# Weight sums of the down projections: made inside DRAM by copies and accumulating transfers, in place of VectorE in SBUF

## The chip, the cores and the metric

The kernel runs on one core of a Trainium2 chip. The core has TensorE (PE, with its weight loads shown apart as PEld), VectorE (DVE), ScalarE (ACT), GpSimd (POOL) and SyncE (SP). In this kernel SP only issues transfers between DRAM and SBUF; POOL does a little arithmetic and can issue transfers too. Each engine works through its own instructions in order and waits for the others at semaphores. The metric is the time of one execution on the device in microseconds, the median of several runs.

## The reference, cut to what matters

A trunk of two layers on a sequence of 1,024 tokens with 1,024 channels. Layer 0 mixes tokens by a gated linear recurrence with 8 heads (HGRN2), layer 1 by attention in a window. Each layer ends with a gated feed-forward part, whose last step is a product with `ffn_w_out`, of 2,816 rows and 1,024 columns:

```python
def conv_ffn(h, w_in, conv_w, conv_b, w_out):
    u = h @ w_in
    ...
    a, b = jnp.split(u, 2, axis=-1)
    return (jax.nn.silu(a) * b) @ w_out
```

Each head of the recurrence ends with a normalisation over its channels:

```python
    o = o * lax.rsqrt(jnp.mean(jnp.square(o), -1, keepdims=True) + RMS_EPS)
```

## The kernel before, in words

**The product with `ffn_w_out`.** It is a Strassen-Winograd product: both matrices are cut into 2 x 2 blocks, and 7 block products stand for 8, at the price of sums of blocks on both sides. Of the weight's four blocks the method needs four sums. They depend on the weights alone, so the kernel makes them at its beginning, long before the first down projection, and keeps them in two DRAM tensors `bsd`, one for each layer, of 128 x 11 x 2 x 1,024 numbers. The class `Down` reads them back (`sum_b`, L560 to L562). `operands` (L564) loads the two operands of a product and forms the activations' sums on VectorE, then splits both into a high and a low part; `evacuate` (L610) adds a product, when it is done, into the output rows `Y`. The products come in the order 1, 2, 5, 6, 7, 3, 4.

**The stage in which the sums are made.** It is the loop over the 8 heads of layer 0. For each head TensorE makes the projections (L194 to L196 and L739, L740) and, put between them, the head's own chain of small products (L200): VectorE multiplies decays into the head's tensors level by level (L1015 to L1020), PE makes scores of them, and so on. At the end of a head's chain VectorE forms `og` (L1111), ScalarE sums its squares (L1123), GpSimd makes 1/rms of them in two small instructions (L1124, L1125), VectorE multiplies it into `og` (L1127), and PE transposes the result (L204).

The order of this stage is written out by a planner, the class `Order`: `t` counts TensorE's time as products are recorded, `v` is the time to which VectorE is booked. A chain goes on when `t` has passed the wait that it gave with `yield`; `od.behind` gives a wait until VectorE's booked work is done. Where VectorE is booked less than 1.5 us ahead, `od.fill` (the function `lay`, L1158) puts in work that can stand anywhere: low parts of weights, and the sums of `ffn_w_out`. The engines themselves know nothing of `t`: on the chip each takes its instructions in the recorded order as soon as their semaphores allow.

**The sums.** `slot_begin` (L1188) is called at the begin of each of 64 slots (8 for each head). The weight is cut into 22 units of 256 rows, 11 for each layer. A slot stores the units that are summed (SP, L1193), loads the next unit into two free rows of `Y` (SP, two transfers, L1200), and puts the four subtractions of a unit loaded two slots ago into `pending`, from which `lay` takes them one by one (VectorE, L1209):

```python
for x, y, z in ((b11, b12, b11), (b12, b22, b12), (b22, b22, b11), (b21, b21, b22)):
    pending.append(lambda x=x, y=y, z=z: tt(x, y, z, op=sub))
```

The same SP queue carries the weights of the heads (L164, tiles `raw`), which ScalarE (L176) and VectorE (L169) split into a high and a low part in `HL`.

Of the kernel before, what the change touches and what calls it, by code (L numbers as in the profile page):

```python
# [107 lines left out]
def trunk(ctx: ExitStack, tc: tile.TileContext, a: dict, out: bass.AP):  # L108
# [429 lines left out]
    class Down:  # L538
# [25 lines left out]
        def operands(self, i, k):  # L564
# [10 lines left out]
            elif p == 5:  # L575
                self.block_a(R[:, 0], k, 1, 0)
                self.block_a(x[:, 0], k, 1, 1)
                self.sum_b(R[:, 1], k, 1)
                tt(R[:, 0], R[:, 0], x[:, 0], op=add)
                x = R  # L580
            elif p == 6:
                self.block_a(x[:, 0], k, 0, 0)
                self.sum_b(R[:, 1], k, 2)
                tt(R[:, 0], R[:, 0], x[:, 0], op=sub)
                x = R
            elif p == 7:
                self.block_a(x[:, 0], k, 1, 1)
                self.sum_b(x[:, 1], k, 3)
                tt(x[:, 0], x[:, 0], R[:, 0], op=sub)
            elif p == 3:  # L590
                self.block_a(x[:, 0], k, 0, 1)
                self.block_b(x[:, 1], k, 1, 1)
                tt(x[:, 0], x[:, 0], R[:, 0], op=sub)
            else:
                self.block_a(x[:, 0], k, 1, 1)
                self.sum_b(x[:, 1], k, 4)
# [13 lines left out]
        def evacuate(self, p, tb, ps, ln):  # L610
            lo, hi = [Y[:, t, :].rearrange("p (h n) -> p h n", h=2) for t in (tb, tb + 4)]
            both = ps.unsqueeze(1).to_broadcast([P, 2, 512])
            if p == 1:
                for y in (lo, hi):
                    nc.vector.scalar_tensor_tensor(y, y, ALPHA, both, op0=ALU.mult, op1=ALU.add)
            elif p in (6, 7):
                tt(hi, hi, both, op=add)
            for y in {2: [lo[:, 0]], 5: [lo[:, 1], hi[:, 1]], 6: [lo[:, 1]], 3: [lo[:, 1]], 4: [hi[:, 0]]}.get(p, []):
                tt(y, y, ps, op=add)

# [57 lines left out]
    with tc.tile_pool(name="t", bufs=1, reuse_waits="tile") as raws, hgrn_pool as hp:  # L678
# [463 lines left out]

        pairs = FF // 256
        lead = [0, 3, 2, 2, 2, 2, 1, 0]
        begins = [4] + [8 * h + lead[h] for h in range(1, NH)]
        free, units, loaded, summed = {r: 0 for r in (0, 2, 4, 6)}, list(range(2 * pairs)), [], []
        slot_no = [-1]
        pending, lowparts, movelows, old = [], [], [], []

# [8 lines left out]
        def lay():  # L1158

            if lowparts and lowparts[0][0] <= od.t:  # L1160
                lay_low()
            elif pending:
                pending.pop(0)()
                od.vec(0.65, 0.0)
            elif movelows and movelows[0][1] <= od.t:
                lay_moved()
            else:
                return False
# [18 lines left out]

        def slot_begin():  # L1188
            slot_no[0] += 1
            n = slot_no[0]  # L1190
            while summed and summed[0][2] < n:
                i, r, _ = summed.pop(0)
                nc.sync.dma_start(bsd[i // pairs][:, i % pairs, :, :], Y[:, r:r + 2, :])  # L1193
                free[r] = n + 1
            rows = [r for r in free if free[r] <= n <= begins[r] + 1]
            if units and rows:
                i, r = units.pop(0), rows[0]
                for k in range(2):
                    row = (k * pairs + i % pairs) * P
                    nc.sync.dma_start(Y[:, r + k, :], a["ffn_w_out"][i // pairs][row:row + P, :])  # L1200
                loaded.append((i, r, n))
                free[r] = 9 * NH
            while loaded and loaded[0][2] <= n - 2:
                i, r, _ = loaded.pop(0)
                blocks = Y[:, r:r + 2, :].rearrange("p a (b n) -> p a b n", b=2)
                (b11, b12), (b21, b22) = [(blocks[:, k, 0], blocks[:, k, 1]) for k in range(2)]

                for x, y, z in ((b11, b12, b11), (b12, b22, b12), (b22, b22, b11), (b21, b21, b22)):
                    pending.append(lambda x=x, y=y, z=z: tt(x, y, z, op=sub))  # L1209
                last = pending.pop()  # L1210
                pending.append(lambda i=i, r=r, last=last: (last(), summed.append((i, r, slot_no[0]))))

# [17 lines left out]
        with tc.manual_schedule(engines={EN.PE, EN.SP, EN.Activation, EN.DVE, EN.Pool}):  # L1230
# [5 lines left out]
            for k in range(4):  # L1236
                slot_begin()
                next(steps)
# [12 lines left out]

            task = od.spawn(all_heads())
            w = nw
            for h in range(1, NH):
# [4 lines left out]
                for k, make in enumerate(((), make_ig[:1], make_ig[1:], ())):  # L1259
                    slot_begin()  # L1260
                    next(steps)
# [11 lines left out]
                for tp in range(NB // 2):  # L1273
                    if tp == lead[h]:
                        ready.append((h, w["out"]))
                    slot_begin()
                    if h == NH - 1 and tp:
# [8 lines left out]
                w = nw  # L1286
            if units or loaded or pending or summed:
                raise ValueError("a unit is left")
# [389 lines left out]
```

## Time and profile before

| | |
|---|---|
| median of 3 runs | 2129.04 us (2128.96 to 2129.31) |
| the profiled execution, first to last instruction | 2126.5 us |
| median less that span | 2.5 us |
| busy: PE, DVE, ACT, POOL | 2116.9, 1765.4, 926.4, 132.7 us |
| the loop over heads and its neighbourhood | 50 to 490 us of the span |
| first down projection ends | about 1160 us |
| granted TensorE clock | 0.999 |

A row of the page or of a view names the line, the engine, the operation, the output and the inputs by the program's names, the shape, and how often (`x88`); then busy time and the mean of one in ns, and what ended the idle time before. A row of the timeline begins with start and duration in us. A row of the stretches gives the stretch, its length, then busy time and number of instructions for PE, PEld, DVE, ACT and POOL, then the granted clock, the share of time in which the DMA engines were busy, and GB/s.

### The profile page before, as it was taken

How to read it: one execution, taken by the hardware profiler on the slowest of the kernel's cores; microseconds unless marked ns; L12 is line 12 of the kernel's file. 1: busy time of each engine (PE TensorE's matmuls, PEld its weight loads, DVE VectorE, ACT ScalarE, POOL GpSimd, SP SyncE). 2: the span in 40 equal slices, each digit the busy share in tenths (PEclk: the TensorE clock that was granted, in tenths of full speed). 3: DMA queues.
4: the chain of work that ended last, by engine and by line, in shares of the span. 5: the costliest groups of instructions: out<-in, count | busy, mean ns of one | idle time of the engine just before them, and what ended most of it. 6: DMA issues, size and time to landing. Idle time of an engine off the chain costs nothing.

```text
span 2126.5 us, 32114 instructions
## 1 busy us (share of the span) xinstructions
PE 2116.9 (100%) x12639; PEld 1776.7 (84%) x12639; DVE 1765.4 (83%) x2378; ACT 926.4 (44%) x1491; POOL 132.7 (6%) x150
## 2 busy tenths in 40 slices
PE   9999999999999999999999999999999999999998
PEld 8888888888888888888888888888888888888887
DVE  4777776677999999888977758969999999878986
ACT  4444444452444444444433356743544444444430
POOL 1000000001100000000001113321000000000002
PEclk9999999999999999999999999999999999999999
DMA  6655443205223222238854511042232222249662
GB/s 218 245 210 168 145 131 120 75 30 180 100 83 98 88 90 80 80 99 272 293 183 166 161 31 41 24 149 90 80 105 94 90 89 80 89 147 334 220 207 97
DMA packets 231566, 280.53 MB, mean 132 GB/s; under 512 B 30152, under 2 KB 160376, under 8 KB 228600
## 3 DMA queue, kind: packets, MB, share of 16 engines
q1 hardware_dynamic: 230464, 278.11, 39.4%
q8 instruction: 99, 1.62, 0.3%
q10 hardware_dynamic: 856, 0.37, 0.1%
q14 instruction: 51, 0.42, 0.1%
q0 software_dynamic: 96, 0.02, 0.0%
HBM read 215.51 MB, written 62.94 MB: 131 GB/s over the span
## 4 chain that ended last, share of the span: by engine, by line
PE 99%; DMA 0%; DVE 0%; SPq 0%; issue 0%; DVEq 0%; ACT 0%; ACTq 0%
PE psmm L194 17%; PE psmm L196 17%; PE psmm L195 17%; PE psax L194 10%; PE psax L195 10%; PE psax L196 10%; PE psmm L739 5%; PE psax L200 4%; PE psmm L740 3%; PE psmm L204 1%; PE psmm L200 1%; PE psax L1452 1%; PE psax L204 1%; PE psmm L1299 1%; PE psmm L777 0%; DMA raw<-in_hgrn_w_in_dram 0%
## 5 line engine op out<-in xcount | busy, mean ns | idle before, releaser
L194 PE MATMUL psmm<-T,HL 128*128 128x512 f32 x768 | 303.5, 395 | 0.0
L196 PE MATMUL psmm<-T,HL 128*128 128x512 f32 x768 | 299.4, 390 | 0.0
L195 PE MATMUL psmm<-T,HL 128*128 128x512 f32 x768 | 299.2, 390 | 0.0
L498 DVE SCALAR_TENSOR_TENSOR Y<-Y,cwt 128x1023 f32<-128x1023 f32 (+1 forms) x176 | 224.9, 1281 | 45.3 <-ACT Y L496 43.9
L221 ACT CAST HL<-rx 128x1024 fp32r<-128x1024 f32 (+1 forms) x151 | 150.7, 1007 | 174.4 <-PE psmm L195 30.4
L169 DVE TENSOR_TENSOR HL<-rx,HL 128x1024 fp32r<-128x1024 f32 (+1 forms) x151 | 178.3, 1187 | 16.5 <-ACT HL L221 16.2
L739 PE MATMUL psmm<-HL,T 128*128 128x512 f32 x496 | 176.8, 399 | 0.0
L196 PEld LDWEIGHTS psmm<-T,HL 128*128 128x128 f32 x768 | 144.2, 188 | 30.5
L194 PEld LDWEIGHTS psmm<-T,HL 128*128 128x128 f32 x768 | 144.3, 188 | 29.7 <-issue 0.4
L195 PEld LDWEIGHTS psmm<-T,HL 128*128 128x128 f32 x768 | 144.4, 188 | 28.8 <-issue 0.4
L496 ACT ACTIVATE Y<-Y,cwt 128x1024 f32<-128x1024 f32 x88 | 108.7, 1238 | 101.5 <-DVE Y L485 89.1
L740 PE MATMUL psmm<-HL,T 128*128 128x256 f32 x496 | 138.9, 280 | 0.0
L194 PE MATMUL psax<-T,HL 128*128 128x512 f32 x352 | 137.3, 390 | 0.0
L196 PE MATMUL psax<-T,HL 128*128 128x512 f32 x352 | 137.0, 389 | 0.0
L195 PE MATMUL psax<-T,HL 128*128 128x512 f32 x352 | 137.0, 389 | 0.0
L243 POOL TENSOR_TENSOR rs<-rs,nhalf 128x1 f32<-128x1 f32 x32 | 44.6, 1396 | 1287.0 <-DVE rs L242 1287.0
L739 PEld LDWEIGHTS psmm<-HL,T 128*128 128x128 f32 x496 | 93.1, 188 | 21.0
L740 PEld LDWEIGHTS psmm<-HL,T 128*128 128x128 f32 x496 | 93.7, 189 | 0.4
L221 ACT CAST HT<-rx 128x1024 fp32r<-128x1024 f32 (+1 forms) x37 | 35.5, 961 | 125.6 <-DVE rx L452 76.7
L169 DVE TENSOR_TENSOR HL<-raw,HL 128x1024 fp32r<-128x1024 f32 x51 | 62.0, 1217 | 21.4 <-ACT HL L176 20.2
L196 PEld LDWEIGHTS psax<-T,HL 128*128 128x128 f32 x352 | 66.1, 188 | 13.6
L195 PEld LDWEIGHTS psax<-T,HL 128*128 128x128 f32 x352 | 66.1, 188 | 13.6
(316 smaller groups left out, 5229.5 us busy)
## 6 DMA issues: line engine op xcount, KB each, us to landing
rx<-in_ffn_w_in_dram SPq DMA_DIRECT2D x136, 256.0 KB, 3.2
rx<-gd SPq DMA_DIRECT2D x118, 256.0 KB, 3.8
Y<-in_ffn_w_out_dram SPq DMA_DIRECT2D x44, 512.0 KB, 6.0
bsd<-Y SPq DMA_DIRECT2D x22, 1024.0 KB, 4.8
gd<-Y SPq DMA_DIRECT2D x44, 512.0 KB, 2.6
rx<-in_ffn_w_out_dram SPq DMA_DIRECT2D x54, 256.0 KB, 4.8
R<-bsd SPq DMA_DIRECT2D x44, 256.0 KB, 5.1
Y<-in_ffn_w_in_dram SPq DMA_DIRECT2D x40, 256.0 KB, 2.9
```

Of the source, the lines that this page charges most:

```text
L169: make = lambda e: e.tensor_tensor(lo, src, hi.bitcast(F32), op=ALU.subtract)
L194: nc.tensor.matmul(ps, st(0), mv(0), start=start, stop=False)
L195: nc.tensor.matmul(ps, st(0), mv(1), start=False, stop=False)
L196: nc.tensor.matmul(ps, st(1), mv(0), start=False, stop=stop)
L200: nc.tensor.matmul(ps, lhsT, rhs, start=start, stop=stop, **kw)
L204: nc.tensor.transpose(ps, src, ident)
L221: nc.scalar.copy(hi, src)
L243: nc.gpsimd.tensor_tensor(rs, rs, nhalf, op=ALU.pow)
L496: nc.scalar.activation(c, u, AF.Identity, bias=cwt[:, l, 3, ci:ci + 1], scale=cwt[:, l, 2, ci:ci + 1])
L498: nc.vector.scalar_tensor_tensor(c[:, sh:], u[:, :S - sh], cwt[:, l, 2 - sh, ci:ci + 1], c[:, sh:], op0=ALU.mult, op1=ALU.add)
L739: nc.tensor.matmul(ps, T[:, 0, kc, ts], w[:, :, kc % 4, :], start=kc == 0, stop=False)
L740: nc.tensor.matmul(ps[:, :256], T[:, 1, kc, ts], w[:, 0, kc % 4, :], start=False, stop=kc == KC - 1)
```

## The change

The four sums of a layer are made in DRAM, from `ffn_w_out` straight into `bsd`. A generator, `down_sums`, is run by the planner beside the heads. For each layer it first records four plain copies of a block, issued by SP, then in three further steps additions: GpSimd issues a transfer with `accum_op=add`, which adds its source to what stands at its destination. Each block of 11 x 128 rows goes in four pieces, of 3, 3, 3 and 2 times 128 rows; the planner books 4.5 us after each piece and 16 us more after each step.

Since these transfers add, the sums that contained differences become pure additions; that is the same method with the signs of two blocks turned, and the signs are put right elsewhere: in the activations' sums (`operands`) and when a product is added into `Y` (`evacuate`), where a product that was added to both halves of a row at once (1,024 columns with the product repeated) is now added to one half and subtracted from the other, in two instructions of 512.

The machinery of slots, units and `pending` goes, and so do the transfers of units through `Y`.

```diff
             elif p == 6:
                 self.block_a(x[:, 0], k, 0, 0)
                 self.sum_b(R[:, 1], k, 2)
-                tt(R[:, 0], R[:, 0], x[:, 0], op=sub)
+                tt(R[:, 0], R[:, 0], x[:, 0], op=add)
                 x = R
...
-            both = ps.unsqueeze(1).to_broadcast([P, 2, 512])
             if p == 1:
                 for y in (lo, hi):
-                    nc.vector.scalar_tensor_tensor(y, y, ALPHA, both, op0=ALU.mult, op1=ALU.add)
-            elif p in (6, 7):
-                tt(hi, hi, both, op=add)
-            for y in {2: [lo[:, 0]], 5: [lo[:, 1], hi[:, 1]], 6: [lo[:, 1]], 3: [lo[:, 1]], 4: [hi[:, 0]]}.get(p, []):
-                tt(y, y, ps, op=add)
+                    for c, op in enumerate((add, sub)):
+                        nc.vector.scalar_tensor_tensor(y[:, c], y[:, c], ALPHA, ps, op0=ALU.mult, op1=op)
+            for y, op in {2: [(lo[:, 0], add)], 5: [(lo[:, 1], sub), (hi[:, 1], sub)],
+                          6: [(hi[:, 0], sub), (hi[:, 1], add), (lo[:, 1], add)], 7: [(hi[:, 0], add), (hi[:, 1], sub)],
+                          3: [(lo[:, 1], sub)], 4: [(hi[:, 0], add)]}.get(p, []):
+                tt(y, y, ps, op=op)
...
-            elif pending:
-                pending.pop(0)()
-                od.vec(0.65, 0.0)
...
+        def down_sums():
+
+            n = FF // 256
+            for l in range(2):
+                wb = a["ffn_w_out"][l].rearrange("(r k p) (c n) -> r c p k n", r=2, k=n, c=2)
+                t1, t3, t4, t2 = [bsd[l][:, :, i, j * 512:(j + 1) * 512] for i in range(2) for j in range(2)]
+                steps = [((t1, wb[0, 0]), (t3, wb[1, 1]), (t2, wb[1, 1]), (t4, wb[1, 0])),
+                         ((t1, wb[0, 1]), (t3, wb[0, 1])), ((t2, t1),), ((t4, t2),)]
+                for i, step in enumerate(steps):
+                    for dst, src in step:
+                        for k0, k1 in ((0, 3), (3, 6), (6, 9), (9, n)):
+                            if i:
+                                nc.gpsimd.dma_start(dst[:, k0:k1], src[:, k0:k1], accum_op=add)
+                            else:
+                                nc.sync.dma_start(dst[:, k0:k1], src[:, k0:k1])
+                            yield 4.5
+                    yield 16.0
...
             task = od.spawn(all_heads())
+            sums = od.spawn(down_sums())
...
-            od.finish([params] + moved[:2])
+            od.finish([params, sums] + moved[:2])
```

How instructions move. On GpSimd, from the sixth head's 1/rms to the eighth's, as it stands now (`ss` is the tile of a head's sums of squares, `bsd_92` the sums of layer 1):

```order
L1124 TENSOR_SCALAR ss<-ss 128x8
L1125 TENSOR_TENSOR ss<-ss,nhalf 128x8
L1193 DMA bsd_92<-in_ffn_w_out_dram 128x3x512 x3
L1193 DMA bsd_92<-in_ffn_w_out_dram 128x2x512
L1193 DMA bsd_92<-in_ffn_w_out_dram 128x3x512 x3
L1193 DMA bsd_92<-in_ffn_w_out_dram 128x2x512
L1124 TENSOR_SCALAR ss<-ss 128x8
L1125 TENSOR_TENSOR ss<-ss,nhalf 128x8
L1193 DMA bsd_92<-bsd_92 128x3x512 x3
L1193 DMA bsd_92<-bsd_92 128x2x512
L1193 DMA bsd_92<-bsd_92 128x3x512 x3
L1193 DMA bsd_92<-bsd_92 128x2x512
```

Before, L1124 and L1125 of all eight heads followed each other with nothing between them. Now eight transfers stand behind the sixth head's pair and eight behind the seventh's; layer 0's stand behind the first head's pair (one), the second's (seven) and the third's (eight).

On VectorE, in the first head's chain, the multiplications of decays (L1015 to L1020; `qp`, `kp`, `tot` are the head's tensors, `Y` the rows that held the units of `ffn_w_out`):

```order
 L1020 TENSOR_TENSOR tot<-fg 128x512
 L1035 TENSOR_TENSOR kd<-kp,qp 128x512 x2
-L1209 TENSOR_TENSOR Y<-Y 128x512
 L1015 TENSOR_TENSOR qp<-qp,tot 128x256x2
 L1017 TENSOR_TENSOR kp<-kp,tot 128x256x2
 L1020 TENSOR_TENSOR tot<-tot 128x256
-L1209 TENSOR_TENSOR Y<-Y 128x512 x2
 L1015 TENSOR_TENSOR qp<-qp,tot 128x128x4
 L1017 TENSOR_TENSOR kp<-kp,tot 128x128x4
 L1020 TENSOR_TENSOR tot<-tot 128x128
```

The subtractions that filled VectorE between the levels of the chain are gone, and the levels follow each other directly.

On SyncE, at the begin of the second head (`raw` are the weights of the heads):

```order
 L164 DMA raw_100<-in_hgrn_w_in_dram 128x4x128 x2
-L1193 DMA bsd_91<-Y 128x2048
-L1200 DMA Y<-in_ffn_w_out_dram 128x1024 x4
-L1193 DMA bsd_91<-Y 128x2048
-L1200 DMA Y<-in_ffn_w_out_dram 128x1024 x2
+L1195 DMA bsd_91<-in_ffn_w_out_dram 128x3x512 x3
+L1195 DMA bsd_91<-in_ffn_w_out_dram 128x2x512
+L1195 DMA bsd_91<-in_ffn_w_out_dram 128x3x512 x2
 L164 DMA raw_101<-in_hgrn_w_in_dram 128x8x128
 L164 DMA raw_99<-in_hgrn_w_in_dram 128x8x128
```

Stores that waited for VectorE's sums and loads that waited for a free row of `Y` make way for six copies that depend on no engine; the next head's weights stand behind them.

More of the change, by code (lines that the diff above doesn't have):

```diff
@@ L578, in operands @@
                 self.sum_b(R[:, 1], k, 1)
-                tt(R[:, 0], R[:, 0], x[:, 0], op=add)
+                tt(R[:, 0], x[:, 0], R[:, 0], op=sub)
                 x = R
@@ L588, in operands @@
                 self.sum_b(x[:, 1], k, 3)
-                tt(x[:, 0], x[:, 0], R[:, 0], op=sub)
+                tt(x[:, 0], R[:, 0], x[:, 0], op=sub)
             elif p == 3:
@@ L592, in operands @@
                 self.block_b(x[:, 1], k, 1, 1)
-                tt(x[:, 0], x[:, 0], R[:, 0], op=sub)
+                tt(x[:, 0], R[:, 0], x[:, 0], op=sub)
             else:
@@ L1138, in norm @@
                     split_scaled(T[:, 0, h, ts], T[:, 1, h, ts], ps[:, ts], par[:, 16:17])
-        pairs = FF // 256
         lead = [0, 3, 2, 2, 2, 2, 1, 0]
[L1145 to L1148, printed above, removed]
+        lowparts, movelows, old = [], [], []
         def lay_low():
@@ L1186, in rest @@
             old[:] = soon
[L1188 to L1211, printed above, removed]
+        def down_sums():
[14 more added lines that the diff above has]
+                    yield 16.0
         def slot_end(wait, *makes):
@@ L1236, in trunk @@
             for k in range(4):
-                slot_begin()
                 next(steps)
@@ L1259, in trunk @@
                 for k, make in enumerate(((), make_ig[:1], make_ig[1:], ())):
-                    slot_begin()
                     next(steps)
@@ L1275, in trunk @@
                         ready.append((h, w["out"]))
-                    slot_begin()
                     if h == NH - 1 and tp:
@@ L1286, in trunk @@
                 w = nw
-            if units or loaded or pending or summed:
-                raise ValueError("a unit is left")
             while lowparts:
```

## The prediction

> **What bounds the kernel now.** I read the page's head and its chain first, then the waits of TensorE, then the stretch of the program in which the sums are made.
>
> ```profile
> span 2126.5 us, 32114 instructions
> PE 2116.9 (100%) x12639; PEld 1776.7 (84%) x12639; DVE 1765.4 (83%) x2378; ACT 926.4 (44%) x1491; POOL 132.7 (6%) x150
> PE 99%; DMA 0%; DVE 0%; SPq 0%; issue 0%; DVEq 0%; ACT 0%; ACTq 0%
> ```
>
> PE is busy for all but 2126.5 - 2116.9 = 9.6 us, and the chain that ended last is PE for 99%. A busy PE is modelled, so I ask next whether PE waited for anybody. This is the whole list of PE's waits over the span:
>
> ```profile
> PE psmm L834 <- DVE Y L785: 1.0, 1, 1.0
> PE psmm L777 <- ACT HL L766: 0.4, 1, 0.4
> PE psmm L777 <- DVE HL L757: 0.3, 1, 0.3
> ```
>
> All three, 1.7 us together, stand at the very start, before the loop over heads in which the sums are made. The stretch that holds this loop, from 50 to 490 us (columns: span, then busy time of PE, weight load, DVE, ACT, POOL):
>
> ```profile
> 50.00:490.00 440.00, 440.00 (x4448) 375.09 (x4447) 313.45 (x569) 196.73 (x435) 14.99 (x16) 1.00 0.43 148
> ```
>
> PE is busy for 440.00 of 440 us at a granted clock of 1.00, while DVE is idle for 126 us of it and the DMA engines for 57%. So the change works on engines that nobody waits for. Its gain is limited by what PE still waits for; its loss is whatever it makes PE wait for.
>
> **VectorE's part.** The removed subtractions, and the evacuations that are split:
>
> ```profile
> L1209 DVE TENSOR_TENSOR Y<-Y 128x512 f32<-128x512 f32 x88 | 60.1, 689 | 1.5
> L615 DVE SCALAR_TENSOR_TENSOR Y<-Y,psmm x16: 1214/1215/1222, 997.2 to 1941.0; 128x1024 f32<-128x1024 f32 x16
> L617 DVE TENSOR_TENSOR Y<-Y,psax x8: 1210/1215/1222, 1093.8 to 2030.7; 128x1024 f32<-128x1024 f32 x8
> L617 DVE TENSOR_TENSOR Y<-Y,psmm x8: 1201/1213/1220, 1118.4 to 2060.9; 128x1024 f32<-128x1024 f32 x8
> L619 DVE TENSOR_TENSOR Y<-Y,psax x24: 670/680/687, 1035.6 to 2092.3; 128x512 f32<-128x512 f32 x24
> 850.00:1160.00 310.00, 310.00 (x1373) 256.92 (x1372) 262.00 (x291) 122.45 (x126) 3.99 (x3) 1.00 0.54 181
> ```
>
> 88 subtractions of 0.689 us go, 60.1 us of DVE in the loop over heads. All of it ran beside a full PE, so it is worth 0 on the path. In the down projections 16 scaled adds and 16 plain adds of 1,024 columns become 64 of 512: 32 x (2 x 0.680 - 1.215) = 4.6 us more DVE, 2.3 us in each layer. The last row is the first layer's down projection with the last third of an up projection: DVE idles 310 - 262 = 48 us there and PE none. The extra 2.3 us is therefore hidden; if that cover were gone it would cost its 2.3 us, twice. The last products, 3 and 4, keep their instructions (a subtraction in place of an addition), so the end of a layer is as before. Sum on DVE: 1765.4 - 60.1 + 4.6 = 1709.9 us busy.
>
> The order of PE moves too, since its planner counted the subtractions as VectorE time: a head's chain of small products now stands earlier by what the planner booked for the subtractions ahead of it, 0.65 us each and up to four, 2.6 us. The same products are issued, so I take 0.
>
> **SyncE's part.** Two loads and a store for each of 22 units go, 32 copies come, mixed with the weight loads of the heads. A load can come late by what is ahead of it on the queue.
>
> ```profile
> 108.08 2.44 SPq L164 DMA_DIRECT2D raw<-in_hgrn_w_in_dram  x4
> 130.43 1.04 ACT L176 CAST HL<-raw 128x1024 fp32r<-128x1024 f32 x1
> DMA to landing us min/median/max: 2.5/3.4/6.2
> q1 hardware_dynamic: 230464, 278.11, 39.4%
> ```
>
> Loads issued by 110.5 us are first used at 130.4, 20 us later, and land in 2.5 to 6.2 us: 14 us to spare at least. The last row (packets, MB, share) gives the engines' pace: 278.11 MB in 39.4% of 2126.5 us is 332 MB per ms when all 16 work. A copy of three blocks, 128 x 3 x 2,048 bytes or 0.79 MB, is 2.4 us at that pace. At most six copies stand in a row ahead of a load: 14 us, if they all come at once. Just covered; I take 0. What the copies need they have: they wait for no engine, so SP runs ahead, and the first sum is wanted by the down projection, hundreds of us later.
>
> **GpSimd's part, which decides.** 32 accumulating transfers stand in POOL's queue, between the steps that turn a head's sum of squares into 1/rms (L1124, L1125). A transfer waits for the copy or the sum that it builds on, and behind it wait L1124, then DVE's scaling of the head (L1127), then PE's transposes (L204). POOL issues one as soon as its inputs have landed, whatever PE is doing. So each gap between two heads must hold its transfers: 1, 7, 8, 0, 0, 8, 8. These are the gaps with 7 or 8 (idle time of POOL in brackets), and the last of L1125's durations:
>
> ```profile
> 208.07 0.20 POOL L1124 TENSOR_SCALAR ss<-ss 128x8 f32<-128x8 f32 x1 [48.05 <-ACT sq L1123]
> 264.62 0.20 POOL L1124 TENSOR_SCALAR ss<-ss 128x8 f32<-128x8 f32 x1 [54.63 <-ACT sq L1123]
> 424.37 0.20 POOL L1124 TENSOR_SCALAR ss<-ss 128x8 f32<-128x8 f32 x1 [48.31 <-ACT sq L1123]
> 477.82 0.20 POOL L1124 TENSOR_SCALAR ss<-ss 128x8 f32<-128x8 f32 x1 [51.53 <-ACT sq L1123]
> 478.10 1.64 POOL L1125 TENSOR_TENSOR ss<-ss,nhalf 128x8 f32<-128x8 f32 x1
> ```
>
> What room follows, DVE's scaling and PE's first weight load of the transposes for the last two heads:
>
> ```profile
> 430.65 1.22 DVE L1127 TENSOR_TENSOR og<-og,ss 128x1024 f32<-128x1024 f32 x1
> 432.97 0.91 PEld L204 LDWEIGHTS psax<-ident,og 128*128 128x128 f32 x8
> 479.77 1.23 DVE L1127 TENSOR_TENSOR og<-og,ss 128x1024 f32<-128x1024 f32 x1 [3.30 <-POOL ss L1125]
> 484.89 1.03 PEld L204 LDWEIGHTS psax<-ident,og 128*128 128x128 f32 x8
> ```
>
> The seventh head's L1125 ends at 424.37 + 0.28 + 1.64 = 426.3: its room is 432.97 - 426.3 - 1.22 = 5.4 us. The eighth's ends at 479.74: 484.89 - 479.74 - 1.23 = 3.9 us.
>
> No accumulating transfer is in the trace. The nearest rows for its time a, with three blocks:
>
> ```profile
> bsd<-Y SPq DMA_DIRECT2D x22, 1024.0 KB, 4.8
> rx<-bsd SPq DMA_DIRECT2D x32, 256.0 KB, 2.9
> 1.24 0.78 POOL L137 DMA_DIRECT2D gd<-in_ln_mix_g_dram  x1 [0.81 <-POOLq L1661]
> 426.00:478.00 52.00, 52.00 (x548) 44.85 (x548) 40.36 (x68) 27.79 (x58) 0.47 (x2) 1.00 0.09 28
> ```
>
> Of the 2.9 us of a 256 KB load (0.26 MB), 0.8 is data at 332 MB per ms, so 2.1 is fixed; POOL's issue takes 0.8. Lower end: POOL goes on once it has issued, a = 0.8. Next: it stands until one pass over 0.79 MB has landed, 0.8 + 2.1 + 2.4 = 5.3. Upper end: the sum reads two blocks for one written, 0.8 + 2.1 + 4.7 = 7.6; a two-block piece is a - 1.5. I take 6.4, the middle of the last two: the 1,024 KB store lands in 4.8 us, and so little else uses the DMA engines in the last gap (9%) that 332, an average over packets of 1.2 KB, understates the pace. A gap of eight then keeps POOL 6a + (a - 1.5) + 0.8 = 7a - 0.7 = 44.1 us before the last is issued, under 48.31: nobody waits. At 7.6 it is 52.5: the seventh head is 4.2 us late, inside its room; the eighth 4.2 + 52.5 - 51.53 = 5.2 late, 1.3 more than its room. So the term is 0, with 1.3 at the upper end.
>
> [...]
>
> **Sum.** 2126.5 of span + 0 (DVE) + 0 (SP) + 0 (POOL) = 2126.5. The runs' median, 2129.04, lies 2.5 above this span; with that, 2129.0 us.
>
> **Rivals.** *POOL comes late (slower).* If the sum in DRAM is dearer than its bytes, L1124 waits and PE with it. From a = 7.5 the eighth head's transposes are late; with S = 7a - 0.7 the last two heads cost 2S - 103.7. At a = 8.6: S = 59.5, 15 us. The third and fourth heads add: 6a - 0.7 in a gap of 48.05, then S in 54.63, with some 3.9 us of room at the end, 13a - 107.9 = 4 us. Together 19 us: 2148. [...] For it: nothing in the trace bounds the adding. Against it: 7.5 is near the end of what bytes give, with all transfers one at a time.
>
> [...]
>
> *PE meets its chain too early (slower).* The planner now places a chain nearer to the VectorE work that it needs. Eight heads with three such places, each late by at most one 0.689 us subtraction's worth: 24 x 0.69 = 17 us, 2146. Against it: no such wait in 440 us now, and VectorE has less to do.
>
> *VectorE's relief helps PE (faster).* PE's own waits bound it at 1.7 us, 2127.3, which is less than can be told. Only if the modelled PE hides waits would it be more: with all 9.6 idle us, 2119.4.
>
> **Chances and range.** Forecast 0.77; POOL late by more than 4.3 us 0.15; chain too early 0.04; relief that shows 0.04. 0.2% is 4.3 us, about what a measurement of this kernel can tell from no change. So faster 0.04, same 0.77, slower 0.19. The range goes from the relief that the waits allow, 2127.3, to a = 8.2 in the first rival (S = 56.7, 9.7 us, the first heads nothing), 2139.0. Beyond it lie some 0.12 above and 0.04 below.
>
> **What would show it.** PE busy between 2116 and 2119 us and no PE wait for DVE L1127 or POOL in the loop over heads; DVE near 1710; L1124 starting within a few us of 208, 265, 424 and 478; the eight transfers of a gap issued over 35 to 53 us. Wrong if L1124 of the last heads ends a long POOL queue, if PE's transposes L204 show a wait, or if PE waits for a weight load behind copies.

## The result, and the profile after

| | before | after |
|---|---|---|
| median of the runs | 2129.11 us (2128.96 to 2129.31) | 2166.2 us (2163.61 to 2168.68) |
| profiled execution, first to last instruction | 2126.5 us | 2161.4 us |
| granted TensorE clock | 0.999 | 0.993 |

The ratio is 1.0174, with a 95% interval of 1.0159 to 1.0188: the change costs 37 us, where the forecast was none and its range ended at 2139.0. The two profiled executions differ by 34.9 us, and nearly all of it is lost between 173 and 525 us of before's time: PE's 101st product of L194 into `psmm` starts 0.8 us later than before, the 201st 10.6, the 301st 34.7, the last 35.2.

The page's head and chain of the changed kernel:

```profile
span 2161.4 us, 32006 instructions
PE 2126.8 (98%) x12639; PEld 1783.8 (83%) x12639; DVE 1713.3 (79%) x2322; ACT 927.1 (43%) x1491; POOL 172.6 (8%) x182
PE 87%; issue 8%; DVE 2%; POOL 2%; DMA 1%; ACT 0%; SPq 0%; DVEq 0%; POOLq 0%; ACTq 0%
```

PE is still what the time is made of, but POOL and "issue" have entered the chain, and PE's own busy time grew by 9.9 us although it issues the same 12639 products. The waits (total, how often, the longest), first PE's, then VectorE's and POOL's:

```profile
PE psax L204 <- DVE og L1127: 23.3, 3, 10.3
PE psmm L194 <- issue: 2.2, 1, 2.2
...
DVE og L1127 <- POOL ss L1125: 36.6, 4, 17.8
...
POOL bsd L1193 <- issue: 189.7, 28, 12.0
```

Read from the bottom: POOL stood 189.7 us before its transfers without waiting for any semaphore, so L1125 of a head came late, so VectorE scaled the head late, so the transposes of three heads kept PE idle for 23.3 us. The timeline of POOL shows it in place; from the third head's 1/rms to the fourth's, and the ends of the two later groups:

```profile
208.82 1.66 POOL L1125 TENSOR_TENSOR ss<-ss,nhalf 128x8 f32<-128x8 f32 x1
213.25 1.30 POOL L1193 DMA_DIRECT2D bsd<-bsd  x1 [2.77 <-issue]
220.88 1.24 POOL L1193 DMA_DIRECT2D bsd<-bsd  x1 [6.32 <-issue]
228.76 1.22 POOL L1193 DMA_DIRECT2D bsd<-bsd  x1 [6.64 <-issue]
...
271.74 1.15 POOL L1193 DMA_DIRECT2D bsd<-bsd  x1 [6.72 <-issue]
272.97 0.19 POOL L1124 TENSOR_SCALAR ss<-ss 128x8 f32<-128x8 f32 x1
...
388.75 1.29 POOL L1193 DMA_DIRECT2D bsd<-in_ffn_w_out_dram  x1
...
447.84 1.14 POOL L1193 DMA_DIRECT2D bsd<-in_ffn_w_out_dram  x1 [8.24 <-issue]
449.06 0.19 POOL L1124 TENSOR_SCALAR ss<-ss 128x8 f32<-128x8 f32 x1
449.33 1.66 POOL L1125 TENSOR_TENSOR ss<-ss,nhalf 128x8 f32<-128x8 f32 x1
454.83 1.31 POOL L1193 DMA_DIRECT2D bsd<-bsd  x1 [3.84 <-issue]
...
513.01 1.15 POOL L1193 DMA_DIRECT2D bsd<-bsd  x1 [12.03 <-issue]
514.24 0.19 POOL L1124 TENSOR_SCALAR ss<-ss 128x8 f32<-128x8 f32 x1
```

The brackets in front of L1124 that showed 48 to 55 us of idle time before are gone: POOL goes from the last transfer straight into a 1/rms that is already late. Eight transfers start over 271.74 - 213.25 = 58.5 us, then 59.1 and 58.2, one every 8.4 us. Even the first of a group waits where another group has just ended (3.84 us ahead of 454.83): the last transfer of that one, issued at 447.84, is still under way (its kind takes a median of 8.1 us to land).

The stretches around the waits of PE (stretch, length, busy time and number of PE, PEld, DVE, ACT, POOL, then the granted clock, DMA share, GB/s):

```profile
276.00:280.00 4.00, 3.78 (x15) 3.48 (x16) 3.97 (x7) 1.42 (x2) 0.00 (x0) 0.57 0.28 50
303.00:307.00 4.00, 4.00 (x12) 2.83 (x10) 0.30 (x1) 0.00 (x0) 0.00 (x0) 0.59 0.68 223
448.00:452.00 4.00, 0.00 (x0) 0.00 (x0) 0.97 (x1) 0.00 (x0) 2.83 (x3) 0.50 0.58 74
452.00:456.00 4.00, 3.69 (x15) 3.41 (x15) 3.93 (x6) 1.11 (x1) 1.17 (x1) 0.50 0.32 57
516.00:520.00 4.00, 2.51 (x10) 2.41 (x11) 1.23 (x1) 0.47 (x1) 0.18 (x1) 0.50 0.91 208
520.00:524.00 4.00, 4.00 (x14) 3.15 (x14) 1.93 (x4) 2.37 (x5) 0.00 (x0) 0.73 0.02 3
```

After these waits (4.45, 2.19, 8.60 and 10.29 us) PE works at half its clock for some us: a 512-column product then starts 0.43 us after the last, not 0.23. The clock is halved for 3.41, 3.41, 10.24 and 10.24 us at these four places, and PE works in 16.5 us of them; as an estimate, that costs 16.5 x (1 - 0.23 / 0.43) = 7.7 us, most of PE's extra 9.9 busy us. Where the rest of the 9.9 lies was not found. Waits of 23.3, a wait of 2.2 at L194 with nothing in the profile that PE waited for (read below as a wait for its own instructions, an inference whose grounds are in the last section), and 9.9 of longer work make 35.4, against 34.9 of span.

The transfers themselves, KB of each and the median from issue to landing:

```profile
bsd<-in_ffn_w_out_dram SPq DMA_DIRECT2D x24, 768.0 KB, 11.4
bsd<-in_ffn_w_out_dram POOLq DMA_DIRECT2D x12, 768.0 KB, 8.1
bsd<-bsd POOLq DMA_DIRECT2D x12, 768.0 KB, 7.5
```

### The profile page after: what moved, and what is told of

It is laid out like the page before. It is cut to its first block, busy times and chain, and to the rows that moved or that the text cites. A ratio compares the mean times of both kernels' runs of the same rounds, so it can differ in the third digit from the quotient of the medians.

```text
span 2161.4 us, 32006 instructions
## 1 busy us (share of the span) xinstructions
PE 2126.8 (98%) x12639; PEld 1783.8 (83%) x12639; DVE 1713.3 (79%) x2322; ACT 927.1 (43%) x1491; POOL 172.6 (8%) x182
## 3 DMA queue, kind: packets, MB, share of 16 engines
q0 software_dynamic: 11872, 23.09, 6.8%
q8 instruction: 99, 1.62, 0.3%
HBM read 238.58 MB, written 86.01 MB: 150 GB/s over the span
## 4 chain that ended last, share of the span: by engine, by line
PE 87%; issue 8%; DVE 2%; POOL 2%; DMA 1%; ACT 0%; SPq 0%; DVEq 0%; POOLq 0%; ACTq 0%
PE psmm L194 16%; PE psmm L196 16%; PE psmm L195 16%; PE psax L194 9%; PE psax L196 9%; PE psax L195 9%; PE psmm L739 3%; PE psax L200 2%; PE psmm L740 1%; PE psmm L200 1%; POOL bsd L1193 1%; PE psmm L204 1%; PE psax L1434 1%; PE psax L204 1%; POOL ss L1125 0%
## 5 line engine op out<-in xcount | busy, mean ns | idle before, releaser
L194 PE MATMUL psmm<-T,HL 128*128 128x512 f32 x768 | 304.2, 396 | 2.2 <-issue 2.2
L194 PEld LDWEIGHTS psmm<-T,HL 128*128 128x128 f32 x768 | 144.6, 188 | 29.7 <-issue 0.4
L194 PE MATMUL psax<-T,HL 128*128 128x512 f32 x352 | 137.3, 390 | 0.0
L194 PEld LDWEIGHTS psax<-T,HL 128*128 128x128 f32 x352 | 66.1, 188 | 13.6
## 6 DMA issues: line engine op xcount, KB each, us to landing
bsd<-in_ffn_w_out_dram SPq DMA_DIRECT2D x24, 768.0 KB, 11.4
```

What stands on the lines that cost most here:

```text
L194: nc.tensor.matmul(ps, st(0), mv(0), start=start, stop=False)
```

## The experiments

The theory after this reading: POOL lets one accumulating transfer through at a time, a group of eight keeps it some 60 us, the 1/rms behind it is late, PE waits, and runs at half clock after. The rivals: the DRAM traffic itself, or the changed order, is what costs, and POOL only shows it. Each run was timed beside runs of the kernel before on the same chip.

| run | median us | before | ratio (95%) |
|---|---|---|---|
| no accumulating transfers | 2131.08 | 2129.18 | 1.0013 (1.0003 to 1.0022) |
| more room for descriptors | 2133.37 | 2129.18 | 1.0021 (1.0012 to 1.0031) |
| transfers that copy | 2134.61 | 2129.18 | 1.0024 (1.0015 to 1.0034) |
| 1/rms on VectorE | 2133.57 | 2129.18 | 1.0021 (1.0012 to 1.0030) |
| transfers spread | 2130.58 | 2128.95 | 1.0010 (1.0001 to 1.0018) |
| spread and more room | 2131.85 | 2128.95 | 1.0016 (1.0007 to 1.0025) |
| order and signs alone | 2128.11 | 2128.95 | 0.9996 (0.9987 to 1.0005) |
| copies in one bunch | 2128.58 | 2128.95 | 0.9999 (0.9990 to 1.0008) |
| POOL held, 66 us | 2191.64 | 2129.16 | 1.0295 (1.0281 to 1.0309) |
| copies of one layer | 2128.53 | 2129.16 | 0.9997 (0.9988 to 1.0006) |
| POOL held, 59 us | 2165.78 | 2129.83 | 1.0173 (1.0159 to 1.0187) |
| POOL held as the transfers did | 2168.37 | 2129.36 | 1.0188 (1.0174 to 1.0202) |
| the extra tile alone | 2136.57 | 2129.88 | 1.0033 (1.0020 to 1.0046) |

**No accumulating transfers.** In `down_sums`:

```diff
-                                nc.gpsimd.dma_start(dst[:, k0:k1], src[:, k0:k1], accum_op=add)
+                                pass
```

> Leaves out the 32 accumulating transfers on POOL's queue (the products then use unsummed blocks); the copies on SP's queue, the turned signs and the new order on every engine stay. Theory (the 1/rms steps stand on POOL behind the transfers; PE idles for them 23.3 us, runs at a halved clock after it, about 10 us): the three waits of the transposes L204 are gone, 1/rms at the times of before, and the time is 2128 to 2133 us; the 2.2 us in which PE waited for instructions beside the copies may stay. Rival (it is the copies' traffic and PE's changed order that cost, and POOL only shows it): 2150 us or more, with waits left on PE that POOL has no part in.

35 of the 37 us are gone. What remains above before, 1.9 us, is one wait of PE:

```profile
PE psmm L194 <- issue: 1.9, 1, 1.9
PE psmm L834 <- DVE Y L785: 1.0, 1, 1.0
...
288.00:292.00 4.00, 4.00 (x160) 3.08 (x159) 0.36 (x1) 0.00 (x0) 0.00 (x0) 1.00 1.05 323
292.00:296.00 4.00, 2.15 (x10) 1.66 (x9) 3.90 (x11) 3.25 (x5) 0.00 (x0) 1.00 1.02 308
```

PE works off 160 small products and as many weight loads in 4 us, then stops, with the DMA engines full (1.05, 1.02) of the second layer's copies: it is busy for 2.15 of the next 4 us.

**More room for descriptors.** (The tile of `pr` is put in a place that is free at that time, and `sk` cut to the columns in use, to make room.) The room is `dynamic_dma_scratch_size`; what lies in it no trace shows.

```diff
-    nc = bacc.Bacc("TRN2", target_bir_lowering=False, num_devices=1, dynamic_dma_scratch_size=1024)
+    nc = bacc.Bacc("TRN2", target_bir_lowering=False, num_devices=1, dynamic_dma_scratch_size=1792)
```

> The room for descriptors of POOL's queue is 1792 bytes of a partition in place of 1024, two small tiles are moved or cut to make place, and nothing else. Theory one (the room holds the descriptors of one three-block transfer, not of two, and POOL stands until the one before has drained): two are under way at once, the spacing of the transfers' issues falls from 8.2 us to 6 or less, and the time to 2130 to 2145 us. Theory two (the transfer itself takes 8 us whatever is queued, two reads and a write by one queue): the spacing stays near 8, two being under way only moves the start by one, and the time stays at 2158 to 2168 us.

Theory one. POOL's timeline in the same gap as above:

```profile
211.46 2.58 POOL L1193 DMA_DIRECT2D bsd<-bsd  x2
219.16 1.23 POOL L1193 DMA_DIRECT2D bsd<-bsd  x1 [5.11 <-issue]
...
244.90 1.15 POOL L1193 DMA_DIRECT2D bsd<-bsd  x1 [1.90 <-DVE Ab L979]
265.61 0.19 POOL L1124 TENSOR_SCALAR ss<-ss 128x8 f32<-128x8 f32 x1 [19.57 <-ACT sq L1123]
```

Two go out at once, eight start over 244.90 - 211.46 = 33.4 us in place of 58.5, and L1124 finds POOL idle for 19.57 us. No head waits for POOL, and one constant of the build has taken back 33 of the 37 us. So it was not the data alone: with 1792 in place of 1024 the next transfer goes out before the last has landed (7.0 to 12.8 us after its issue), and eight are issued in 33.4 us.

**Transfers that copy.**

```diff
-                                nc.gpsimd.dma_start(dst[:, k0:k1], src[:, k0:k1], accum_op=add)
+                                nc.gpsimd.dma_start(dst[:, k0:k1], src[:, k0:k1])
```

> The 32 transfers on POOL's queue copy and do not add (the sums are then wrong: the last source alone), with the same bytes written, at the same places. If reading the destination as a second source is what sets a transfer's time: the spacing falls by a third to a half, to 4 to 5.5 us, a group of eight takes 32 to 44 us, no head waits and the time is 2129 to 2135 us. If a transfer's time is the fixed part and POOL's descriptors: the spacing stays at 7 to 8.5 us and the time at 2155 to 2168 us.

Eight start over 231.43 - 211.82 = 19.6 us, faster than either side had it; no head waits.

```profile
211.82 1.56 POOL L1193 DMA_DIRECT2D bsd<-bsd  x2
217.34 0.74 POOL L1193 DMA_DIRECT2D bsd<-bsd  x1 [3.96 <-issue]
...
231.43 0.69 POOL L1193 DMA_DIRECT2D bsd<-bsd  x1 [2.87 <-DVE tot L1020]
```

Two go out at once although the room is the old one, and an issue costs 0.7 us where an addition costs 1.2. How long the plain transfers take to land, then GpSimd's own DMA queue (packets, MB, share of the 16 engines), here and in the changed kernel:

```profile
bsd<-in_ffn_w_out_dram POOLq DMA_DIRECT2D x12, 768.0 KB, 6.5
bsd<-bsd POOLq DMA_DIRECT2D x12, 768.0 KB, 6.0
q0 software_dynamic: 6240, 23.09, 3.2%
q0 software_dynamic: 11872, 23.09, 6.8%
```

So the adding costs twice here: 1.5 to 1.6 us more to land for each, and one at a time (58.5 us for eight). With two at a time in both, additions take 33.4 / 19.6 = 1.7 times as long as copies. The queue's rows fit both: the same 23.09 MB go in nearly twice as many packets when they are added, 2 KB each where the copies' are 4 KB. If the room goes by packets, one addition fills that of two copies; this is the author's inference from these rows, and no run varied the packets' size alone.

**1/rms on VectorE.** In `norm`:

```diff
-            nc.gpsimd.tensor_scalar(ss, ss, 1.0 / P, RMS_EPS, op0=ALU.mult, op1=ALU.add)
-            nc.gpsimd.tensor_tensor(ss, ss, nhalf.to_broadcast([P, NB]), op=ALU.pow)
+            nc.vector.tensor_scalar(ss, ss, 1.0 / P, RMS_EPS, op0=ALU.mult, op1=ALU.add)
+            nc.vector.tensor_tensor(ss, ss, nhalf.to_broadcast([P, NB]), op=ALU.mult)
```

> All transfers stay, but the two small steps of 1/rms are VectorE's and not POOL's (the power -1/2 is left out there, a product with -0.5 stands in its place, so the heads' scale is another). Theory (POOL's order is what delays the heads): the transfers keep their spacing of about 8 us, no transpose waits for POOL, and the time is 2128 to 2133 us. Rival (the transfers' and copies' traffic slows loads or the instruction fetch): the time stays above 2145 us although no head waits for POOL.

The transfers keep their 8 us (issues at 377.26, 385.25, 393.12 us), and PE's list has no wait for L1127:

```profile
PE psmm L196 <- issue: 2.8, 1, 2.8
PE psax L200 <- issue: 1.2, 1, 1.2
```

The same traffic with nobody behind it on POOL costs 4.4 us, and the two waits for instructions are 4.0 of them. Theory, 0.6 us above its range, with the rival right for these 4 us.

**Transfers spread.** Copies and additions are put in two lists; the first layer's copies go out 3 us apart in the plan, then, in turn, one addition and one copy of the second layer:

```diff
+            while adds:
+                d, x = adds.pop(0)
+                nc.gpsimd.dma_start(d, x, accum_op=add)
+                yield 10.4 / 2
+                if copies:
+                    nc.sync.dma_start(*copies.pop(0))
+                yield 10.4 / 2
```

> The same copies and accumulating transfers at other places: the 32 transfers stand 10.4 us apart in the plan, so that 4, 4, 5, 5, 5, 4 and 5 of them lie between the heads' 1/rms steps in place of 1, 7, 8, 0, 0, 8 and 8, and the copies of the second layer are issued between them, two or three at a time. Room for descriptors as in the changed kernel. Theory (only a group that outlasts its head's stage delays anything): spacing still about 8 us, five of them 41 us of the some 53 us between heads, no transpose waits for POOL, the PE stays at full clock and the time is 2128 to 2132 us. Rival (accumulating transfers cost PE time wherever they lie): 2140 us or more.

The five of the fourth gap, with the old room, and the 1/rms behind them:

```profile
269.08 1.30 POOL L1198 DMA_DIRECT2D bsd<-bsd  x1
277.74 1.23 POOL L1198 DMA_DIRECT2D bsd<-bsd  x1 [7.36 <-issue]
...
303.95 1.22 POOL L1198 DMA_DIRECT2D bsd<-in_ffn_w_out_dram  x1 [8.67 <-DVE tot L1020]
323.23 0.19 POOL L1124 TENSOR_SCALAR ss<-ss 128x8 f32<-128x8 f32 x1 [18.06 <-ACT sq L1123]
```

Still 8.7 us each, and 18.06 us to spare. The transfers' time matters only where a group outlasts its gap. 2130.58 us is the best that a version with the sums made in DRAM reached, 1.6 us above before; PE has three waits for instructions of 2.5 us together.

**Spread and more room.** Both edits; on top of the one just shown:

```diff
-    nc = bacc.Bacc("TRN2", target_bir_lowering=False, num_devices=1, dynamic_dma_scratch_size=1024)
+    nc = bacc.Bacc("TRN2", target_bir_lowering=False, num_devices=1, dynamic_dma_scratch_size=1792)
```

> The spread places and the larger room for descriptors together. Theory: as with the spread places alone, 2128 to 2131 us, since the room then buys nothing that anyone waits for; spacing of the issues follows the plan, about 10 us. If the wait of PE for instructions comes from copies issued in bunches of seven, it is under 0.5 us here. Rival (that wait comes from anything that loads DRAM): still 2 to 3 us, and 2131 to 2134 us. Nothing here can go below 2127, since PE stays busy as before.

As forecast, the room buys nothing once nobody waits. The waits for instructions are 2.4 us, and 2131.85 us lies above the theory's range and inside the rival's: these waits do not come from bunches of copies alone. The forecast that the issues would follow the plan's 10 us failed too: two went out at once, the others 3 to 9 us apart.

**Order and signs alone.** Neither copies nor additions, and in `Down`:

```diff
-            self.w, self.sums, self.tasks, self.ahead = a["ffn_w_out"][l], bsd[l], [], []
+            self.w, self.sums, self.tasks, self.ahead = a["ffn_w_out"][l], a["ffn_w_out"][l].rearrange("(r k p) c -> p k r c", r=2, p=P), [], []
```

> Neither copies nor accumulating transfers: only the turned signs, VectorE without the 88 subtractions, and the new order (the products read blocks of the weight itself in place of the sums). Theory (the relief of VectorE and the order are worth nothing on a path that is PE's): VectorE 1710 us busy, PE as before, 2128 to 2130.5 us, within 0.1% of before. Rival (the changed order costs by itself): over 2132 us; rival (the relief is worth something): under 2127 us.

2128.11 us, in the interval with 1: the moved chains, VectorE's 52 us of relief and the split evacuations are worth nothing that can be told. PE's complete list of waits is at the start of the program:

```profile
PE 2117.0 (100%) x12639; PEld 1776.5 (84%) x12639; DVE 1713.6 (81%) x2322; ACT 927.5 (44%) x1491; POOL 132.8 (6%) x150
PE psmm L834 <- DVE Y L785: 1.0, 1, 1.0
PE psmm L777 <- ACT HL L766: 0.9, 1, 0.9
```

**Copies in one bunch.** No additions, and:

```diff
-                            yield 4.5
+                            if i or not l:
+                                yield 4.5
```

> The accumulating transfers left out, and the 16 copies of the second layer issued on SP's queue in one bunch in place of 1, 7, 5 and 3. Theory (PE's wait of 2 us for instructions is their fetch standing behind copies that are queued): 16 copies take about 37 us to land, and waits for instructions, or for the weights loaded behind the bunch, come to 4 to 20 us, with a halved clock after each: 2135 to 2155 us. Rival (the wait belongs to that place of the program, whatever is queued): one wait of 2 to 3 us near 294 us as with the smaller bunches, 2130 to 2132 us.

My theory of bunches fell: 16 copies in a row make one wait of 1.3 us at 294 us, less than bunches of seven (1.9), and 2128.58 us. The rival had the place right and the size too large. The run does not show that the length of the queue is without effect: the bunch was issued from 249.5 to 279.2 us, and with a copy landing 12.4 us after its issue (median) most of it had, as an estimate, landed by 292.

**Copies of one layer.** Order and signs alone, with the first layer's copies put back:

```diff
+                            if not i and not l:
+                                nc.sync.dma_start(dst[:, k0:k1], src[:, k0:k1])
```

> The first layer's 16 copies alone, no accumulating transfers and no copies of the second layer (the products read blocks of the weight itself). Theory (PE waits for its instructions at 294 us because transfers of DRAM are queued there): with the second layer's copies gone that wait is under 0.3 us, and the time is 2127.5 to 2129 us, that of the order and signs alone. Rival (what the first layer's copies move is late later on): a wait of over 1 us stays near 294 us.

PE has no wait for instructions at all and 2128.53 us. So the wait at 294 us stands only in runs with transfers under way just then; those of the first layer, elsewhere in the program, make none. A dense run of small products stands before it (160 in 4 us without additions, 187 from 290 to 300 us in the changed kernel), and the shorter waits in the runs with POOL's transfers (at most 1.1 to 1.4 us) stand at L200, the line of the heads' small products.

**POOL held.** Neither copies nor additions; where each addition stood, POOL computes on a small tile of its own:

```diff
+                                for _ in range(5 if k1 - k0 == 3 else 3):
+                                    nc.gpsimd.tensor_tensor(held, held, nhalf.to_broadcast([P, NB]), op=ALU.pow)
```

> No copies and no accumulating transfers (the products read blocks of the weight itself); in the place of each accumulating transfer POOL computes for about as long as it was held: five small powers of 1.66 us for three blocks, three for two, so a group of eight holds it 59.8 us as the transfers did (59.6). Theory (the time is the hold of POOL, PE's wait and its halved clock after it, nothing of DRAM's traffic): the waits of the transposes at the fourth, seventh and eighth head are back with 20 to 27 us, the clock is at half for 15 to 30 us after them, and the time is 2156 to 2164 us. Rival (the transfers' traffic has a part of its own, over 10 us of the 37): 2140 to 2152 us. Rival (the clock's drop comes from the transfers and not from PE's wait): the waits are back, the clock stays at 1.0, 2148 to 2154 us.

The hold came out too long: 36 powers in a row took 65.94 us, not 59.8, so four heads wait (39.7 us) and the time is far above the forecast. The second of these runs has four powers for every addition:

```diff
-                                for _ in range(5 if k1 - k0 == 3 else 3):
+                                for _ in range(4):
```

> As the run before in which POOL computed in the transfers' place, but the hold is set by what that run measured of such a power standing in a row (36 in 65.94 us, 1.83 us each): four for every transfer, so seven transfers' places hold POOL 51 us (the transfers held it 49.3) and eight hold it 58.6 us (59.6). No copies and no transfers. Theory (POOL's hold, PE's wait and its halved clock after that are all but 2 to 3 us of the 35): waits of 3 to 6, 7 to 10 and 8 to 11 us before the transposes of the fourth, seventh and eighth head, the clock at half for 15 to 30 us after them, 28 to 36 us lost by the end of the heads, 2155 to 2165 us. Rival (the transfers' traffic has over 10 us of the 35 for itself): under 25 us lost, 2140 to 2153 us.

Waits of 15.9 us, 24.5 us lost by the end of the heads (the 321st product of L194 into `psmm`; 34.7 in the changed kernel): just under the mark that I had set for the traffic, while 2165.78 us lies far above the rival's range. But it held POOL 59.5, 57.6 and 59.6 us from one 1/rms to the next where the transfers took 62.5, 60.2 and 63.2, and the loss grew by 12 us more in the FFNs. Hence a third, with 27, 34, 33 and 34 powers in the four gaps and a tile of 64 bytes in place of 32:

```diff
-        held = sm.tile([P, NB], F32, name="held", bufs=1)
+        held = sm.tile([P, 2 * NB], F32, name="held", bufs=1)[:, :NB]
+        powers = [4] * 7 + [3] + [5, 5] + [4] * 6 + [5] + [4] * 7 + [5, 5] + [4] * 6
...
-                                for _ in range(4):
+                                for _ in range(powers.pop(0)):
```

> POOL computes in the transfers' place as before, with two corrections. The powers between two heads' 1/rms steps are 27, 34, 33 and 34 at 1.83 us, which is what lay between those steps with the transfers (49.2, 62.5, 60.2 and 63.2 us). And the tile they work on has 64 bytes of a partition in place of 32: in the two runs before, the loss grew by a further 12 us in the two FFNs (every 512-column matmul there some 3 us in 100 longer), where POOL does nothing of it, and a tile of 32 bytes that moves all others by half of 64 is the suspect. No copies and no transfers. Theory: 4 to 7, 7 to 11 and 9 to 13 us of waits at the fourth, seventh and eighth head, 29 to 36 us lost by the end of the heads, no growth after that, 2157 to 2166 us. If the growth is the hold's own doing it is there again, and the time is 2168 to 2178 us. If the transfers' traffic has a large part, under 25 us are lost by the end of the heads.

Its waits, and the clock in two of the places:

```profile
PE psax L204 <- DVE og L1127: 23.2, 3, 10.6
...
276.00:280.00 4.00, 3.56 (x16) 3.29 (x17) 3.96 (x7) 1.42 (x2) 0.00 (x0) 0.59 0.00 0
509.00:513.00 4.00, 1.81 (x9) 1.82 (x10) 1.22 (x1) 0.00 (x0) 0.87 (x1) 0.50 0.00 0
```

23.2 us of waits against 23.3 with the transfers, and the halved clock behind them with the DMA engines idle (0.00): the hold alone makes both, and no traffic is needed for either. 28.1 us are lost by the end of the heads, just under the 29 to 36 forecast. The growth in the FFNs was smaller (8 us, not 12), but there, so the forecast that 64 bytes would end it failed, and 2168.37 us lies in the range given for that case. The last run has the tile and no powers:

```diff
-        powers = [4] * 7 + [3] + [5, 5] + [4] * 6 + [5] + [4] * 7 + [5, 5] + [4] * 6
+        powers = [0] * 32
```

> The kernel of the run before with the tile of 64 bytes and no power on POOL (one clearing of the tile is left): neither hold, copies nor transfers. If the growth of 8 to 12 us in the two FFNs belongs to the extra tile, which moves the tiles allocated after it, it is there again: 2134 to 2141 us, and the loss by the end of the heads under 1 us. If it belongs to the hold of POOL (or to PE's waits): none of it, 2127.5 to 2129.5 us.

The growth is the tile's: 0.2 us ahead of before at the end of the heads, 8.1 behind at the end. In the stretch from 580 to 980 us 1751 products pass where 1766 did, with no wait between them:

```profile
580.00:980.00 400.00, 400.00 (x1751) 328.43 (x1750) 362.56 (x399) 175.09 (x192) 4.82 (x2) 1.00 0.29 92
```

Each of the two runs against its own runs of before, the hold alone is worth (2168.37 - 2129.36) - (2136.57 - 2129.88) = 32.3 us of the 37, if the tile costs the same with and without it. Some 4.8 us are left. The runs with all the transfers and nobody waiting for POOL lie 4.2 to 5.4 us above before, which fits, or 1.6 and 2.9 where the transfers are spread.

No version tried is faster than the kernel before by more than can be told: with no sums to make at all the time is that of before.

## Why the prediction was wrong

**The bound: right.** PE sets the time, and all that mattered was whether something would make it wait.

**VectorE's part: right.** 1709.9 us was forecast and 1713.3 measured. The removed subtractions gave nothing, the split evacuations cost nothing:

```profile
L615 DVE SCALAR_TENSOR_TENSOR Y<-Y,psmm x32: 675/679/687, 1032.4 to 1976.1; 128x512 f32<-128x512 f32 x32
```

They take the 0.68 us that was assumed, and order and signs alone cost nothing. That settles the rivals "chain too early" and "relief helps PE" as well: neither.

**SyncE's part: the term 0 held for what it spoke of**, the loads: PE has no wait for a load behind copies. A copy landed in 11.4 us (median), with several under way at once; the pace of 332 MB per ms was nearly right (308 to 323 in the stretches with the engines full of copies). The part left out PE's waits for "issue", read here as waits for its instructions: 2.2 us here, 1.3 to 4.1 in the runs with traffic of the second layer or of POOL.

**GpSimd's part: the step that failed.** The mechanism was the one described, and its time a for a three-block addition was mis-sized: 6.4 us chosen, 7.6 the upper end. The formula S = 7a - 0.7 runs from the first issue to the end of the last: 271.74 + 1.15 - 213.25 = 59.6 us measured, so a = (59.6 + 0.7) / 7 = 8.6, beyond the point of decision, 7.5. The term put at 0 became 23.3 us of waits. Two of its parts were low: the issue (1.2 us, not 0.8), and "fixed part plus bytes", taken from loads of SP's queue. A plain copy of POOL's own queue lands in 6.0 to 6.5 us, where 0.8 left off from 5.3 gave 4.5. Adding brings 7.5 to 8.1. That transfers would go strictly one at a time was the assumption behind the upper end, and it held with the room of 1024 (one every 8.4 us); with 1792 eight take 33.4 us, below the 44.1 that the forecast allowed, and the time comes within 4.4 us of the forecast.

**The first rival: right in its place, short in its price.** It was given 0.15. It had worked out this very a: 15 + 4 = 19 us at 8.6, 2148; the waits are 23.3. It left out that a group begins late when the group before has only just been issued (3.84 us ahead of 454.83), which is nearly the difference. And it priced a wait at its own length. Here PE's busy time grew by four tenths of the waits' length, 9.9 us on 25.5, most of it at the halved clock. (The range's upper end, a = 8.2, adds up to 2138.7 and not 2139.0; nothing hangs on that.)

The row of 276 to 280 us, a clock of 0.57 right after 4.45 us without work, shows what PE's idling adds. The prediction had no price for it, though its rival was made of it; in the trace of before there was none to read, with no wait of PE in the loop over heads and a clock of 1.00.

Behind the forecast's a also stood, as the author's estimate, that an addition reads two blocks for one written. No run shows the second read: the page counts 238.58 MB read and 86.01 written with additions and with copies in their place alike. What the runs show is 1.7 times the copies' time with two under way, in packets of half the size. Nor does VectorE's work show in it: an issue of the changed kernel took 1.13 to 1.36 us throughout, and POOL's idle time before its transfers that the profile puts down to "issue" fell from 189.7 to 79.3 us with more room and the same VectorE work.

## What to carry to other kernels

An instruction that issues a transfer can hold its engine, here GpSimd, as long as a transfer lasts (one addition every 8.4 us, at 7.5 to 8.1 us to land): before putting transfers on an engine that also computes, multiply the landing time by the number between two steps that somebody waits for, ask how many can be under way at once, and spread them or give them room if the product is near the gap. Where a PE that is never idle would have to wait, price waits of 2 to 14 us, as an estimate from four runs, at 1.2 to 1.5 times their length (in the runs with POOL held 28.1 us lost on 23.2 of waits, 50.4 on 39.7 and 24.5 on 15.9; 35.4 on 25.5 with the transfers). And where the price of the deciding unit has no row in the trace and is chosen only 15% under the point of decision, the range has to reach well past that point.

## What the runs showed of the hardware

- **A halved clock comes with PE's waits.** In the changed kernel the granted clock is 0.50 for 3.41, 3.41, 10.24 and 10.24 us, beside waits of 4.45, 2.19, 8.60 and 10.29 us. These spells begin 4.6, 3.1, 3.4 and 4.7 us after PE's work stops, the first two with PE back at work, the last two still in the wait. No run tells what sets their length. In the run with copying transfers the clock is 0.50 after a wait of 3.0 us:

```profile
295.00:298.00 3.00, 0.69 (x4) 0.41 (x3) 2.81 (x8) 1.84 (x3) 0.00 (x0) 1.00 0.99 281
298.00:301.40 3.40, 2.69 (x7) 2.10 (x7) 0.00 (x0) 0.00 (x0) 0.00 (x0) 0.50 0.98 337
```

- **A queue of the kind "instruction" shares the DMA engines.** In the page of the changed kernel it moved 1.62 MB in 99 packets, 16 KB each, 0.3% of the 16 engines' time. PE's 12639 products and as many loads are 255 to a packet, so the queue is taken to be PE's, an inference; then, as an estimate, the stretch with 160 products and 159 loads in 4 us uses a packet in 3.2 us. In the changed kernel such a packet starts at 300.54 us, PE's work stops at 300.57, and PE goes on at 302.76; that it waits for this packet is inferred from that. With order and signs alone two such packets pass from 289 to 295 us, with no other traffic, and PE has no such wait; in the seven runs with copies of the second layer these waits are 1.3 to 4.1 us together.
- **A tile of 64 bytes that hardly anything uses cost 8.1 us** between the profiled executions (6.7 between the medians on one chip), in products whose start-to-start grew by about 1% in the FFNs, with no wait. With one of 32 bytes the growth was 12, in the two runs that also held POOL (437 to 438 products in 100 us of the first FFN where the changed kernel has 443: about 1 in 100 longer, not the 3 of the expectation). Why is open; no run tried where a tile lies. The changed kernel has no such growth: its loss stays at 35.2 us from 583 to 2110 us.
